# Latent attention with the rope query's high and low parts stacked in one operand and half of its heads' rope made in the loop; forgetting attention with padded keys and the decay added by VectorE

## The chip, the cores and the metric

The kernel runs on one core of one Trainium2 chip. The metric is the device time of one execution in microseconds; lower is better. The engines have queues of their own: PE (TensorE, matrix products, with its weight loads listed as PEld), DVE (VectorE), ACT (ScalarE), POOL (GpSimd) and SP (SyncE, which only issues DMAs here). An engine runs its queue in order, and an instruction waits at the head of its queue until what it reads is there.

## The reference, cut to what matters

The program is a decoder trunk of two layers on 256 tokens of width 1024, all in float32. A layer is: half a SwiGLU feed-forward (2816 wide), an attention mixer, another half feed-forward, and a gated per-layer embedding, each followed by a layer norm. Layer 0's mixer is forgetting attention (FoX, 16 heads of 64), layer 1's is latent attention (MLA, 16 heads, 128 numbers without position and 64 rotated by rope, with one rotated key for all heads).

```python
def fox_mixer(x, w_in, b_f, w_o):
    h = x @ w_in                                  # q, k, v and one gate logit a head
    cum = jnp.cumsum(jax.nn.log_sigmoid(f_logit), axis=1).transpose(0, 2, 1)
    ...
        s = jnp.einsum('bqhd,bkhd->bhqk', qb, k).astype(jnp.float32) * scale
        return s + cb[:, :, :, None] - cum[:, :, None, :]

def mla_mixer(x, w_dq, q_norm, w_uq, w_o, k_nope, k_rope, v, cos, sin):
    c_q = rms_norm(x @ w_dq, q_norm)
    q = jnp.einsum('bsc,chd->bshd', c_q, w_uq)
    q_nope = q[..., :QK_NOPE_DIM]
    q_rope = rope(q[..., QK_NOPE_DIM:], cos[:, None, :], sin[:, None, :])
    ...
        s = jnp.einsum('bqhd,bkhd->bhqk', qn, k_nope) + jnp.einsum('bqhr,bkr->bhqk', qr, k_rope)
```

Softmax over the keys up to the query's own place follows, then the product with v and with w_o.

## The kernel before, in words

**Precision by parts.** PE works on float32r operands. Every operand is held as a high part (an ACT copy to float32r) and a low part (a DVE subtraction of the high part from the source); `parts` makes such a pair, and `mm3` forms a product as three matmuls into one PSUM bank: high by high, high by low, low by high.

**Weights.** `Stream` loads weights of HBM by DMA from the SP queue into three raw buffers, up to three groups ahead, and splits each piece into its parts in one of about ten buffers (`hl`, and `ota`, `otb`, `qk`, `fs` when they are lent). A split of 1024 columns is one ACT and one DVE instruction (lines 164 and 165). The order of everything is the order in which the Python code emits it; the only planner is `pump`, which after each product emits the next split if its own clock says that ACT and DVE are free. `S.hold` turns it off.

**FoX.** Heads go in pairs, j = 0 to 7. `gen_k(j)` and `gen_q(j)` make the pair's keys and queries (24 matmuls each), head 0 in partitions 0 to 63 and head 1 in 64 to 127. `QK(j)` has a bank for each head: first a product with `sel` and `negc` that adds minus 8 times the decay of the keys, and then six matmuls a head with 64 partitions each. `softmax(j)` adds the causal mask and takes the row's maximum on DVE (line 954), corrects it by the query's decay `cq` (two small DVE instructions a head), takes the exponentials on ACT and divides on POOL. `T(j)` transposes the weights on PE, `AV(j)` multiplies with v. The decays come from `gates()`: a product and then a chain of ACT, POOL and DVE steps, emitted one by one (`bg`) whenever a weight is used. The iteration j is: gen_k(j+1), T(j-1), QK(j), softmax(j), gen_q(j+1), AV(j-1).

**MLA.** Ahead of the loop over heads stand `dq(t)` (the query latent of token block t, then its norm), `V(g, t)` (values of four heads), `cq_transpose(t)`, `q_rope(t)` (the 16 heads' rope queries of block t: two banks, 18 matmuls, then three DVE instructions and an addition on POOL or DVE a bank), `transposed` (eight PE transposes of them and their parts into `xT`), and `gen(0)`, `gen(1)` (`gen` makes a head's key and query without position). The loop over heads h is: gen(h+1), T(h-1), QK(h), softmax(h), O(h-2), at some heads V, AV(h-1). `QK(h)` is an `mm3` on `qk` and an `mm3` on the rope parts `xT` and `kr`, for queries 0 to 127 (128 keys) and 128 to 255 (256 keys). The rope operands hold two heads in their 128 partitions; `kr[s]` is zero in the other head's half. `softmax(h)` takes the maximum (line 1263) and the exponentials (line 1267), and emits the division (POOL, line 1274) at once; `O` is the output product. PSUM has rings of banks: `y` (4), `h` (2), `tr` (2); QK and T share `tr`, gen, AV and V share `h`.

Of the kernel before, what the change touches and what calls it, by code (L numbers as in the profile page):

```python
# [52 lines left out]
VT = {0: (2, (0,)), 5: (2, (1,)), 8: (3, (0,)), 10: (3, (1,))}  # L53
# [201 lines left out]
WIDTH = {"kd": 1280, "dq": 1536, "kq": 1280, "kvv": 1024, "ff": 1024}  # L255


def group_of(key):
    k = key[0]
    if k in ("win", "fv", "kd", "dq"):  # L260
        return key[:-1] + (key[-1] // 2,)
    if k in ("wout", "fk", "fq", "fo", "pg", "pp", "mo", "qr"):
        return key[:-1] + (key[-1] // 2,)
    if k in ("kvk", "qn"):
        return ("kq", key[-1])
    return key


def unit_of(key, raw):
# [4 lines left out]
    if k in ("wout", "fo", "pg", "pp", "mo", "qr"):  # L274
        return raw[:, 1024 * u : 1024 * u + 1024], 128, 1024
# [17 lines left out]
def make_loads(a):  # L293
# [3 lines left out]
    def loads(q, g, raw, fine, between):  # L297
# [41 lines left out]
        elif k == "qr":  # L339
            w = a["mla_w_uq"][0]  # L340
            for s in range(2):
                kk = 2 * i + s
                if kk < 3:
                    q.dma_start(
                        raw[:, 1024 * s : 1024 * s + 1024].rearrange("p (h d) -> p h d", d=64),
                        w[128 * kk : 128 * kk + 128, :, 128:192],
                    )
# [31 lines left out]
class Trunk:  # L379
    def __init__(self, nc, pools, a, S, rec):  # L380
        self.nc, self.a, self.S = nc, a, S
        self.sb, self.ps = pools
        self.rec = rec
        self.bg = deque()
        self.setup()
# [418 lines left out]
    def fox(self, li):  # L804
# [26 lines left out]
        bf = self.tl([128, 1], F32, "bf", 1)  # L831
        sel = self.tl([128, 16], F32R, "sel", 1)
        negc = self.tl([128, 384], F32R, "negc", 1)
        cq = self.tl([128, 16, 2], F32, "cq", 1)
        fr = slice(96, 128)
        nc.gpsimd.memset(bf, 0.0)
        if not self.rec:
            self.dma(bf[112:128, :], a["fox_b_f"][0].rearrange("(p o) -> p o", o=1))
        nc.gpsimd.memset(fs, 0.0)
        nc.gpsimd.memset(negc.bitcast(F32), 0.0)  # L840
        sf = fs[:, 1792:1808]
        nc.gpsimd.tensor_tensor(sf, self.ident[:, 16:32], self.ident[:, 48:64], op=ALU.add)
        nc.gpsimd.tensor_tensor(sf, sf, self.ident[:, 80:96], op=ALU.add)
        nc.gpsimd.tensor_tensor(sel, sf, self.ident[:, 112:128], op=ALU.add)
# [3 lines left out]
        m8 = fs[fr, 1536:1792]  # L848

        def gates():  # L850
# [3 lines left out]
            def s1():  # L854
                nc.scalar.activation(f, ps[fr, 0:256], AF.Identity, bias=bf[fr, :])
                nc.scalar.activation(ab, f, AF.Abs)
# [6 lines left out]
            def s2():  # L863
# [3 lines left out]
                nc.gpsimd.tensor_tensor(u, e, ab, op=ALU.subtract)  # L867
# [3 lines left out]
            def s3():  # L871
                nc.vector.scalar_tensor_tensor(f, f, 0.0, u, op0=ALU.min, op1=ALU.add)
                nc.vector.tensor_tensor_scan(sc[fr, :], f, r, 0.0, op0=ALU.add, op1=ALU.add)
                nc.gpsimd.tensor_scalar(m8, sc[fr, :], -8.0, 1.0, op0=ALU.mult, op1=ALU.mult)
                self.S.busy(dve=600)

            def s4():
                nc.scalar.activation(negc[fr, 0:128], m8[:, 0:128], AF.Copy)
                nc.scalar.activation(negc[fr, 128:384], m8, AF.Copy)

            def s5():
                nc.vector.tensor_tensor(
                    negc[64:96, 128:384], m8, negc[fr, 128:384].bitcast(F32), op=ALU.subtract
                )
                nc.vector.tensor_copy(negc[64:96, 0:128], negc[64:96, 128:256].bitcast(F32))
                self.S.busy(dve=400)

            def s6():
                nc.vector.tensor_copy(negc[0:64, :], negc[64:128, :].bitcast(F32))

            rest = lambda: None
            self.bg.extend((s1, rest, rest, s2, rest, rest, s3, rest, s4, s5, s6))

        def gates_transpose():
            tr = self.bank("tr")
            for t in range(2):
                self.transpose(tr[:, 128 * t : 128 * t + 128], sc[:, 128 * t : 128 * t + 128])
            nc.vector.tensor_copy(
                cq.rearrange("p h t -> p t h"),
                tr[:, 0:256].rearrange("p (t c) -> p t c", c=128)[:, :, 112:128],  # L900
            )
# [8 lines left out]
        qk = self.own([128, 2, 2, 512], F32R, "qk")  # L910
        OT = [self.own([128, 4, 2, 256], F32R, tag) for tag in ("ota", "otb")]

        def gen(j, key, c0, at={}, hold=False):
            ps = self.bank("h")
            ws((key, j), ps[:, 0:256], at, hold)
            o = qk[:, j % 2]
            self.parts(o[:, 0, c0 : c0 + 256], o[:, 1, c0 : c0 + 256], ps[:, 0:256])

        def gen_k(j):
            gen(j, "fk", 256, {0: S.split_now} if j >= 2 else {}, j >= 2)  # L920

        def gen_q(j):
            gen(j, "fq", 0, {}, j >= 2)

        def QK(j, ring):
            sb = [self.bank(ring) for _ in range(2)]
            half = [slice(0, 64), slice(64, 128)]
            o = qk[:, j % 2]
            for s in range(2):
                h = 2 * j + s  # L930
                self.mm(
                    sb[s][:, 0:384], sel[half[s], h : h + 1].to_broadcast([64, 128]), negc[half[s], :],
                    True, False,
                )
            for n, (i, jj) in enumerate(((0, 0), (0, 1), (1, 0))):
                for q0, c0, c1 in ((0, 0, 128), (128, 128, 384)):
                    for s in range(2):
                        self.mm(
                            sb[s][:, c0:c1], o[half[s], i, q0 : q0 + 128],
# [509 lines left out]
```

## Time and profile before

| | |
|---|---|
| median of 3 runs | 1095.18 us (1095.08 to 1095.76) |
| the profiled execution | 1095.58 us, its span from the first to the last instruction 1093.6 us, the other 2.0 us lie around it |
| granted TensorE clock | 0.997 of full speed |
| PE busy | 98% of the span |
| FoX, about | 198 to 312 us of the span |
| MLA, about | 717 to 872 us of the span |

A row of the timeline gives the start, the time that the row covers, engine, line, operation, out<-in, shapes and how many instructions it merges; behind it in brackets stands how long its engine had been idle and what ended that. Matmuls are pipelined: the end of one overlaps the start of the next, so what a matmul costs is read from start to start.

### The profile page before, as it was taken

The page shows a single profiled execution, that of the slowest core. Times are in us where ns is not written, and L with a number is a line of the kernel's source. Part 1 is how long each engine was busy: PE and PEld are TensorE (multiplying, and loading weights), DVE is VectorE, ACT ScalarE, POOL GpSimd, SP SyncE. Part 2 cuts the span into 40 slices and gives each one's busy share as a digit, 9 for nine tenths or more (in the row PEclk, how much of TensorE's full clock was granted, in tenths as well). Part 3 has the DMA queues.
Part 4 walks back from the last instruction along what each step waited for, and adds up shares of the span by engine and source line. Part 5 has one row for each costly group of instructions (what it writes and reads, how often), then busy time and mean ns, then how long its engine had stood idle before and what let it go on. Part 6 is the DMA issues. An engine that isn't in the chain of part 4 may idle for free. (4 is left out here: it accounts for less than half of the span.)

```text
span 1093.6 us, 17616 instructions
## 1 busy us (share of the span) xinstructions
PE 1072.9 (98%) x7148; PEld 970.6 (89%) x7148; DVE 712.1 (65%) x1010; ACT 539.3 (49%) x787; POOL 81.3 (7%) x129
## 2 busy tenths in 40 slices
PE   9999999999999999999999999998999999999996
PEld 6989999899889999988899899987899789898985
DVE  5765545788797545449976454487766886454567
ACT  5564433666645444443664353345655474344431
POOL 0000000322200000001420000011111000000000
PEclk9999999999999999999999999999999999999998
DMA  8896652444358866545577664353533678555502
GB/s 276 279 297 225 205 186 92 155 154 156 119 173 286 269 210 198 187 140 164 171 257 266 193 193 148 103 145 113 155 116 116 202 257 294 165 192 192 192 1 77
DMA packets 150960, 200.04 MB, mean 183 GB/s; under 512 B 11872, under 2 KB 128608, under 8 KB 150880
## 3 DMA queue, kind: packets, MB, share of 16 engines
q1 hardware_dynamic: 150880, 198.92, 56.1%
q8 instruction: 56, 0.92, 0.3%
q14 instruction: 24, 0.20, 0.1%
HBM read 197.85 MB, written 1.05 MB: 182 GB/s over the span
## 5 line engine op out<-in xcount | busy, mean ns | idle before, releaser
L165 DVE TENSOR_TENSOR hl<-raw,hl 128x1024 fp32r<-128x1024 f32 (+3 forms) x285 | 331.6, 1182 | 172.9 <-ACT hl L164 172.0
L164 ACT ACTIVATE hl<-raw 128x1024 fp32r<-128x1024 f32 (+3 forms) x285 | 284.4, 1019 | 197.5 <-PE y L464 83.3
L464 PE MATMUL h<-xT,hl 128*128 128x256 f32 x2064 | 243.7, 278 | 1.0 <-DVE qk L474 0.6
L464 PEld LDWEIGHTS h<-xT,hl 128*128 128x128 f32 x2064 | 238.3, 188 | 2.4 <-DVE qk L474 0.8
L464 PE MATMUL y<-hl,g 128*128 128x512 f32 x804 | 186.6, 390 | 0.0
L464 PEld LDWEIGHTS y<-hl,g 128*128 128x128 f32 x804 | 150.1, 188 | 30.7
L464 PE MATMUL tr<-xT,hl 128*128 128x256 f32 x840 | 98.9, 277 | 0.0
L464 PEld LDWEIGHTS tr<-xT,hl 128*128 128x128 f32 x840 | 96.9, 188 | 0.1
L464 PE MATMUL h<-hl,xT 128*128 128x512 f32 (+1 forms) x396 | 95.1, 389 | 1.1 <-DVE hl L165 0.9
L464 PEld LDWEIGHTS h<-hl,xT 128*128 128x128 f32 x396 | 71.9, 188 | 17.9 <-DVE hl L165 3.4
L536 POOL TENSOR_TENSOR rs<-ve,mhalf 128x1 f32<-128x1 f32 x16 | 14.8, 923 | 822.7 <-DVE ve L535 809.1
L464 PE MATMUL y<-hl,xT 128*128 128x512 f32 (+2 forms) x276 | 57.8, 363 | 0.0
L464 PEld LDWEIGHTS y<-hl,xT 128*128 128x128 f32 x276 | 47.5, 188 | 7.4
L474 DVE TENSOR_TENSOR g<-P,g 128x512 fp32r<-128x512 f32 x36 | 24.9, 693 | 34.4 <-ACT g L473 34.4
L473 ACT ACTIVATE g<-P 128x512 fp32r<-128x512 f32 x36 | 22.7, 632 | 39.9 <-DVE P L643 29.0
L473 ACT ACTIVATE xT<-tr 128x512 fp32r<-128x512 f32 x36 | 20.0, 596 | 37.3 <-PE tr L468 37.1
L464 PE MATMUL y<-hl,ota 128*128 128x512 f32 x144 | 36.1, 394 | 0.0
L165 DVE TENSOR_TENSOR otb<-raw,otb 128x1024 fp32r<-128x1024 f32 (+1 forms) x20 | 24.1, 1203 | 18.2 <-ACT otb L164 18.2
L165 DVE TENSOR_TENSOR qk<-raw,qk 128x1024 fp32r<-128x1024 f32 x21 | 25.7, 1224 | 15.4 <-ACT qk L164 15.4
L164 ACT ACTIVATE qk<-raw 128x1024 fp32r<-128x1024 f32 x21 | 22.2, 1058 | 19.3 <-PE tr L464 6.6
L464 PE MATMUL tr<-xT,otb 128*128 128x256 f32 x264 | 31.7, 276 | 0.0
L464 PEld LDWEIGHTS tr<-xT,otb 128*128 128x128 f32 x264 | 30.7, 188 | 0.0
(230 smaller groups left out, 1374.7 us busy)
## 6 DMA issues: line engine op xcount, KB each, us to landing
raw<-in_ffn_w_in_dram SPq DMA_DIRECT2D x172, 512.0 KB, 4.9
raw<-in_ffn_w_out_dram SPq DMA_DIRECT2D x44, 1024.0 KB, 5.2
raw<-in_fox_w_in_dram SPq DMA_DIRECT2D x12, 1024.0 KB, 5.2
raw<-in_ple_w_gate_dram SPq DMA_DIRECT2D x8, 1024.0 KB, 5.1
raw<-in_mla_w_o_dram SPq DMA_DIRECT2D x8, 1024.0 KB, 5.1
gb<-in_ln_g_dram SPq DMA_DIRECT2D x8, 512.0 KB, 7.3
gb<-in_ln_b_dram SPq DMA_DIRECT2D x8, 512.0 KB, 8.1
raw<-in_fox_w_o_dram SPq DMA_DIRECT2D x4, 1024.0 KB, 5.0
```

Of the source, the lines that this page charges most:

```text
L164: nc.scalar.activation(hi[:, c], src[:, c], AF.Copy)
L165: nc.vector.tensor_tensor(lo[:, c], src[:, c], hi[:, c].bitcast(F32), op=ALU.subtract)
L464: self.nc.tensor.matmul(out, lhsT, rhs, start=start, stop=stop)
L473: self.nc.scalar.activation(hi, src, AF.Copy)
L474: self.nc.vector.tensor_tensor(lo, src, hi.bitcast(F32), op=ALU.subtract)
L536: nc.gpsimd.tensor_tensor(rs, ve, self.mhalf, op=ALU.pow)
```

## The change

**MLA.** The rope query's operand now holds, for one head, its high part in one half of the partitions and its low part in the other; the key's high part stands in both halves (`kr[0]`), its low part in one (`kr[1]`, `kr[2]`), so that the rope product takes two matmuls instead of three. `q_rope` works by token block and half of the heads (n): heads 0 to 7 ahead of the loop, heads 8 to 15 inside it (products at h = 0 and 1, `rotate` behind them, transposes `rope_T` at h = 3 and 5). The weights for it are loaded in other groups. In the loop, gen(h+1) and T(h-1) now stand behind QK(h) and its maxima; the exponentials, the low part of T's copy and the division follow separately, and `S.hold` keeps weight splits out until gen(h+1) is emitted. V(1,0) uses the `y` ring, V(2) is made ahead of the loop, V(3) at h = 7 and 9, and the layer norm's gain is loaded at h = 9. The latent query (`cqt`) lies in `fall`'s buffer.

**FoX.** The key operand `kz` has a zero half for each head, so that a query of both heads (`qq`, 128 partitions) gives one head's scores: QK is six matmuls with 128 partitions into two banks. The decay no longer goes through PE: `gates()` ends by storing 8 times the cumulated decay in DRAM (`decay`), from which four broadcast DMAs fill `fall` (four heads each); `mask_fall` applies the causal mask on POOL, and the DVE instruction of the maximum adds `fall` or `tri` instead of the mask. `sel`, `negc`, `cq` and their instructions go, and the two reciprocals of a pair become one.

```diff
-            self.bg.extend((s1, rest, rest, s2, rest, rest, s3, rest, s4, s5, s6))
...
+                self.dma(decay, sc[112:128, :])
+                load_fall(0)
+                load_fall(1)
+                mask_fall(0)
+            self.bg.extend((s1, rest, s2, rest, rest, s3))
+        def load_fall(g):
+            if not self.rec:
+                d = decay[4 * g : 4 * g + 4, :]
+                self.dma(
+                    fall[:, g % 2].rearrange("p h c -> p (h c)"),
+                    bass.AP(tensor=d.tensor, offset=d.offset, ap=[[0, 128], [1, 1024]]),
+                )
+        def mask_fall(j):
+            h = slice(2 * (j % 2), 2 * (j % 2) + 2)
+            a, b = fall[:, j // 2 % 2, h], tri[:, j // 2 % 2, h]
+            for out, src in ((b, a[:, :, 0:128]), (a[:, :, 128:256], a[:, :, 128:256])):
+                nc.gpsimd.affine_select(
...
         def QK(j, ring):
             sb = [self.bank(ring) for _ in range(2)]
-            for s in range(2):
-                h = 2 * j + s
+            q, k = qq[:, j % 2], kz[:, j % 2]
+            pairs = lambda ap: ap.rearrange("p (s c) -> p s c", s=2)
+            for n, (i, jj) in enumerate(((0, 0), (0, 1), (1, 0))):
                 self.mm(
-                    sb[s][:, 0:384], sel[half[s], h : h + 1].to_broadcast([64, 128]), negc[half[s], :],
-                    True, False,
+                    pairs(sb[0][:, 0:256]), q[:, i, 0:128], pairs(k[:, jj])[:, :, 0:128], n == 0, n == 2
                 )
             for n, (i, jj) in enumerate(((0, 0), (0, 1), (1, 0))):
-                for q0, c0, c1 in ((0, 0, 128), (128, 128, 384)):
-                    for s in range(2):
-                        self.mm(
-                            sb[s][:, c0:c1], o[half[s], i, q0 : q0 + 128],
-                            o[half[s], jj, 256 : 256 + c1 - c0], False, n == 2 and q0 > 0,
-                        )
+                self.mm(sb[1], q[:, i, 128:256], k[:, jj], n == 0, n == 2)
...
+        def rope_T(t, n, ring="tr"):
+            tr = self.bank(ring)
+            for i in range(4):
+                self.transpose(tr[:, 128 * i : 128 * i + 128], z[n][t][:, 128 * i : 128 * i + 128])
+            src = tr.rearrange("p (k c) -> p k c", c=128)
+            half = [slice(64 * s, 64 * s + 64) for s in range(2)]
+            o = [self.xT[:, t, s, 4 * n : 4 * n + 4, :] for s in range(2)]
+            for s in range(2):
+                nc.scalar.activation(o[s][half[s]], src[half[s]], AF.Copy)
+            for s in range(2):
+                nc.vector.tensor_tensor(
+                    o[s][half[1 - s]], src[half[s]], o[s][half[s]].bitcast(F32), op=ALU.subtract
+                )
...
-                self.mm3(
-                    b[:, c0:c1], lambda i: self.xT[:, q0 // 128, i, pair, :],
-                    lambda i: kr[:, i, 0:w], False, True,
-                )
+                r = self.xT[:, q0 // 128, h % 2, h // 2, :]
+                self.mm(b[:, c0:c1], r, self.kr[0][:, 0:w], False, False)
+                self.mm(b[:, c0:c1], r, self.kr[1 + h % 2][:, 0:w], False, True)
...
         for h in range(16):
-            if 1 <= h < 15:
+            S.hold = True
+            QK(h)
+            softmax(h)
+            if h >= 1:
+                T(h - 1)
+            exps(h)
+            if h >= 1:
+                T_low(h - 1)
+            divide(h)
+            if h == 0:
+                gen_q(1)
+            elif h < 15:
                 gen(h + 1)
+            S.hold = False
+            if h == 0:
+                q_rope(0, 1)
+            if h == 1:
+                rotate(0, 1)
+                q_rope(1, 1)
...
+            if h in (3, 5):
+                rope_T(h // 2 - 1, 1, "h")
+            if h in VT:
+                V(*VT[h])
+            if h == 9:
+                self.load_gb(li, 1)
             if h == 15:
                 S.lend("qk")
                 O(LATE, (1,))
-            if h >= 1:
-                T(h - 1)
-            QK(h)
-            softmax(h)
             if h >= 2:
                 O(h - 2, (0, 1) if h - 2 < LATE else (0,))
...
             if h >= 1:
                 AV(h - 1)
+            if h == 1:
+                rotate(1, 1)
```

The next rows are instruction queues in the order in which the program holds them (line, operation, out<-in, shape of the output, how many in a row); the number behind a name counts buffers. First PE in MLA, ahead of the loop, before: `gb` is the latent query's buffer, `ota` the rotated rope queries, `tr<-qk` and `tr<-fs,xT` are QK(0), whose rope keys lie in `fs`.

```order
L464 MATMUL y<-hl_7096,gb 128x512 x6
L468 MATMUL tr<-ident,ota 128x128 x8
L464 MATMUL h<-fs,hl_7111 128x256 x6
L464 MATMUL h<-gb,hl_7125 128x256 x9
L464 MATMUL h<-hl_6949,fs 128x512 x6
L468 MATMUL tr<-ident,ota 128x128 x8
L464 MATMUL h<-fs,hl_7111 128x256 x6
L464 MATMUL h<-gb,hl_7125 128x256 x9
L464 MATMUL tr<-qk 128x128 x3
L464 MATMUL tr<-fs,xT 128x128 x3
L464 MATMUL tr<-qk 128x256 x3
L464 MATMUL tr<-fs,xT 128x256 x3
```

The same stretch of PE in the changed program, where `fall` is the latent query's buffer:

```order
L467 MATMUL h<-fs,hl_7036 128x256 x12
L467 MATMUL y<-hl_6928,fall 128x512 x6
L467 MATMUL y<-hl_7005,fall 128x512 x3
L467 MATMUL h<-fall,hl_7050 128x256 x9
L471 MATMUL tr<-ident,ota 128x128 x4
L467 MATMUL y<-hl_7064,fs 128x512 x6
L471 MATMUL tr<-ident,ota 128x128 x4
L467 MATMUL y<-hl_7064,fs 128x512 x6
L467 MATMUL tr<-qk 128x128 x3
L467 MATMUL tr<-fs,xT 128x128 x2
L467 MATMUL tr<-qk 128x256 x3
L467 MATMUL tr<-fs,xT 128x256 x2
```

The transposes of the rope queries (`tr<-ident,ota`) are 8 instead of 16 and have a product of V behind each four, the gen of head 0 stands ahead of them, gen(1)'s query has moved behind QK(0), and QK(0)'s rope rows are 2 and 2 instead of 3 and 3.

Now DVE in the loop, around head 2, before: the first four rows are softmax(2)'s maxima, `su` the division's reciprocal, `hl` are weight splits, `ota` is AV(1)'s low part, `qk` the low part of gen(4), `PT` that of T(2).

```order
L1263 ISA tr,nm<-tr,mask 128x128
L1263 ISA nm 128x1
L1263 ISA tr,nm<-tr,mask 128x256
L1263 ISA nm 128x1
L1272 RECIPROCAL su<-su 128x2
L165 TENSOR_TENSOR hl_7469<-raw,hl_7469 128x1024
L165 TENSOR_TENSOR hl_7484<-raw,hl_7484 128x512
L474 TENSOR_TENSOR ota<-h,ota 128x256
L165 TENSOR_TENSOR hl_7497<-raw,hl_7497 128x768
L165 TENSOR_TENSOR hl_7508<-raw,hl_7508 128x1024
L474 TENSOR_TENSOR qk<-h,qk 128x512
L474 TENSOR_TENSOR PT<-tr,PT 128x384
```

The same engine in the changed program around head 2:

```order
L1288 ISA tr,nm<-tr,mask 128x128
L1288 ISA nm 128x1
L1288 ISA tr,nm<-tr,mask 128x256
L1288 ISA nm 128x1
L1322 TENSOR_TENSOR PT<-tr,PT 128x384
L1305 RECIPROCAL su<-su 128x2
L477 TENSOR_TENSOR qk<-h,qk 128x512
L165 TENSOR_TENSOR hl_7403<-raw,hl_7403 128x512
L165 TENSOR_TENSOR hl_7409<-raw,hl_7409 128x768
L165 TENSOR_TENSOR hl_7420<-raw,hl_7420 128x1024
L477 TENSOR_TENSOR ota<-h,ota 128x256
```

`PT` (T(1)'s low part) now stands between the maxima and the reciprocal, the low part of `qk` is that of the next head, gen(3), behind this head's reciprocal instead of a head ahead, and the splits come behind it.

Last PE in FoX, around QK of a pair in the loop, before: `tr<-ident,P` is T of the pair before, `y<-negc,sel` and `y<-qk` are QK, `h<-xT` is a gen.

```order
L991 MATMUL tr<-ident,P 128x128 x4
L468 MATMUL tr<-ident,P 128x128 x2
L464 MATMUL y<-negc,sel 128x384 x2
L464 MATMUL y<-qk 128x128 x2
L464 MATMUL y<-qk 128x256 x2
L464 MATMUL y<-qk 128x128 x2
L464 MATMUL y<-qk 128x256 x2
L464 MATMUL y<-qk 128x128 x2
L464 MATMUL y<-qk 128x256 x2
L464 MATMUL h<-xT,hl_2051 128x256 x24
```

And the same PE rows in the changed program, where `qk` holds the padded keys and `qq` the queries:

```order
L986 MATMUL tr<-ident,P 128x128 x4
L471 MATMUL tr<-ident,P 128x128 x2
L467 MATMUL y<-qk,qq 128x256 x3
L467 MATMUL y<-qk,qq 128x512 x3
L467 MATMUL h<-xT,hl_2059 128x256 x24
```

The two products with `negc` and the twelve of 64 partitions have become three of 256 columns and three of 512.

More of the change, by code (lines that the diff above doesn't have):

```diff
@@ L909, in fox, with gen_k @@
         st, PT = {}, {}
-        qk = self.own([128, 2, 2, 512], F32R, "qk")
         OT = [self.own([128, 4, 2, 256], F32R, tag) for tag in ("ota", "otb")]
-        def gen(j, key, c0, at={}, hold=False):
+        def gen_k(j):
             ps = self.bank("h")
[L915 to L920, printed above, removed]
+            ws(("fk", j), ps[:, 0:256], {0: S.split_now} if j >= 2 else {}, j >= 2)
+            o = kz[:, j % 2]
+            part = [(slice(64 * s, 64 * s + 64), slice(256 * s, 256 * s + 256)) for s in range(2)]
+            for r, c in part:
+                nc.scalar.activation(o[r, 0, c], ps[r, 0:256], AF.Copy)
+            for r, c in part:
+                nc.vector.tensor_tensor(o[r, 1, c], ps[r, 0:256], o[r, 0, c].bitcast(F32), op=ALU.subtract)
+            self.S.busy(act=600, dve=600)
```

260 lines of the change are left out of this document (138 added, 122 removed).

## The prediction

> **What bounds the kernel now.** I read the page's engine sums first, then busy time by stretch, then PE's waits, and last the timeline at each wait.
>
> ```profile
> span 1093.6 us, 17616 instructions
> PE 1072.9 (98%) x7148; PEld 970.6 (89%) x7148; DVE 712.1 (65%) x1010; ACT 539.3 (49%) x787; POOL 81.3 (7%) x129
> ```
>
> PE is busy for 98% of the span, so only two things shorten the kernel: fewer or shorter matmuls, and the removal of the few waits of PE. DVE, at 65%, is next. The two stretches of latent attention are where PE is not full (stretch, its length, then us busy and instructions of PE, its weight loads, DVE, ACT and POOL, the granted clock, the DMA engines' busy share, GB/s):
>
> ```profile
> 716.70:748.00 31.30, 28.85 (x155) 24.25 (x155) 28.66 (x47) 14.59 (x26) 6.02 (x7) 1.00 0.57 165
> 748.00:859.00 111.00, 106.44 (x730) 96.57 (x730) 74.56 (x165) 66.71 (x148) 13.63 (x32) 1.00 0.40 123
> ```
>
> The first is MLA ahead of its loop, the second the loop: 2.5 and 4.6 us without PE work. In the first DVE is busy for 28.7 of 31.3 us, so there DVE sets the pace with PE; in the loop it has a third of its time left. What PE waits for in MLA (total, times, longest):
>
> ```profile
> PE tr L468 <- POOL P L1274: 1.7, 3, 0.8
> PE tr L464 <- DVE g L474: 1.2, 1, 1.2
> PE tr L468 <- DVE xT L474: 1.2, 1, 1.2
> PE h L464 <- DVE PT L474: 1.1, 1, 1.1
> PE tr L468 <- DVE PT L1166: 0.8, 1, 0.8
> PE h L464 <- DVE g L474: 0.4, 1, 0.4
> ```
>
> A wait costs more than the idle time listed, since the pipeline runs empty:
>
> ```profile
> 743.98 1.55 PE L464 MATMUL h<-hl,fs 128*128 128x512 f32 x6
> 746.71 1.16 PE L468 MATMUL tr<-ident,ota 128*128 128x128 f32 x8 [1.18 <-DVE xT L474]
> ```
>
> Six matmuls of 512 columns take 6 x 0.233 us from start to start (next fence), so the transposes could have begun at 745.38 and began at 746.71: 1.33 lost for 1.18 idle. I add 0.15 us to each wait.
>
> **MLA, rope product: -3.7 us.** The price of a matmul is read from start to start in QK(0):
>
> ```profile
> 749.69 0.45 PE L464 MATMUL tr<-qk 128*128 128x128 f32 x3
> 749.98 0.50 PE L464 MATMUL tr<-fs,xT 128*128 128x128 f32 x3
> 750.32 0.57 PE L464 MATMUL tr<-qk 128*128 128x256 f32 x3
> 750.72 0.51 PE L464 MATMUL tr<-fs,xT 128*128 128x256 f32 x3
> 751.07 1.56 PE L464 MATMUL tr<-hl,fs 128*128 128x512 f32 x6
> 752.47 0.87 PE L464 MATMUL h<-fs,hl 128*128 128x256 f32 x6
> ```
>
> Three of 128 columns on the rope operands take 0.34 us, three of 256 take 0.35, six of 512 take 1.40: 0.113, 0.117 and 0.233 each. A head loses one of the first and one of the second: 0.23 us, times 16 heads 3.7 us, all on the full engine.
>
> **FoX, QK: -1.6 us.** A pair of heads in the loop before:
>
> ```profile
> 243.47 0.38 PE L468 MATMUL tr<-ident,P 128*128 128x128 f32 x2
> 243.78 0.44 PE L464 MATMUL y<-negc,sel 64*128 64x384 f32 x2
> 244.06 0.85 PE L464 MATMUL y<-qk 64*128 64x128 f32 x12
> 244.84 0.39 PE L464 MATMUL h<-xT,hl 128*128 128x256 f32 x1
> ```
>
> QK takes 244.84 - 243.78 = 1.06 us, and the two transposes ahead of it 0.31, where two at 0.113 would take 0.23: about 0.1 us is lost when PE goes from 128 to 64 partitions, and perhaps as much on the way back, which no row shows by itself. After: three of 256 and three of 512, 3 x 0.117 + 3 x 0.233 = 1.05 us, and no switch. The gain a pair lies between 0.1 (one switch) and 0.2 (both); I take 0.2, since the trace has both switches, so 8 x 0.2 = 1.6 us. The Trainium skill, "TensorEngine Tiling (Array Packing)", Theoretical Speedup, says that a contraction of 64 or less may run up to two times faster as row tiles. By that rule the 3072 columns (2 x 384 and 12 of 128 or 256) should take half of 3072 x 0.455 ns, 0.70 us, the padded form would cost 0.35 us more a pair, and the sum below would end 4.4 us higher. The trace disagrees in size: 1.06 us. The same page says that a change of tiling mode drains the engine (Key Properties); the 0.1 us agree.
>
> The two transposes of `gates_transpose` go as well: -0.3 us by the 0.31 above.
>
> **FoX, the start: about zero.** PE waits there once for the low part of gen(0), queued on DVE:
>
> ```profile
> 224.71 0.50 PE L464 MATMUL h<-xT,hl 128*128 128x256 f32 x2 [0.60 <-DVE qk L474]
> 219.22 0.69 DVE L873 TENSOR_TENSOR_SCAN fs<-fs 32x256 f32<-32x256 f32 x1
> 229.02 0.30 DVE L954 CUSTOM_DVE_ANT_0 y<-y,mask 128x128 f32<-128x128 f32 x1 [0.34 <-PE y L464]
> 232.96 1.63 POOL L976 TENSOR_SCALAR P<-P,su 128x128 f32<-128x128 f32 x4 [11.52 <-DVE su L973]
> 234.49 0.60 PE L991 MATMUL tr<-ident,P 128*128 128x128 f32 x4
> ```
>
> The three DVE steps that build `negc` go, so the 0.6 + 0.15 goes: -0.8. In its place stands a new wait. The maxima of pair 0 (229.02) now need `fall`: the scan's end, the store of `decay`, a broadcast load and two masks on POOL. The nearest DMAs and the nearest mask:
>
> ```profile
> bf<-in_fox_b_f_dram SPq DMA_DIRECT2D x1, 0.1 KB, 1.5
> DMA to landing us min/median/max: 4.0/7.7/9.7
> L437 POOL TENSOR_SCALAR_AFFINE_SELECT mask<-mask x2: 292/293/294, 4.2 to 4.4; 128x128 f32<-128x128 f32 x2
> ```
>
> The second row is that of the sixteen `gb` loads, which also broadcast 512 KB. The scan ends at 219.9 now; the steps between are emitted one weight use earlier, so 1.4 us earlier at best. 218.5 to 219.9, plus 1.5 to 2, plus 4.0 to 9.7, plus 2 x 0.6 (twice the mask's columns): 225.2 to 232.8. PE will end QK(0) near 228 (its wait and two transposes are gone). So the delay is 0 to 4.8 us; the middle, a load of 6 to 7 us, gives about 1, which I take. It reaches PE at once: T(0) begins at 234.49 while POOL ends its divisions at 234.59. The other three loads have a whole pair (8.5 us) or more. On SP the store and the loads stand between weight loads, which then wait for the scan; FoX needs 1 MB in some 8 us, and three buffers cover that. The masks take POOL 1.2 us a pair beside 1.6 of division: hidden. gen_k's parts become two ACT and two DVE instructions, the correction by `cq` (four) goes: even, and hidden under PE. Sum of the start: -0.8 + 1.0.
>
> **MLA, ahead of the loop: -2.5 us.** V(1,0) in the `y` ring no longer waits for a bank: -0.4 - 0.15. cq_transpose(1) has 15 matmuls of 512 (3.4 us) behind dq(1) instead of 12 (2.7), and the wait was 0.8 + 0.15: about -0.9. The rope transposes wait 1.33 for the bank that DVE empties late; now a V product (1.4 us) stands behind each four, and half of the DVE work of rope is left to the loop: -1.3. Fewer waits mean that PE comes sooner to what DVE makes, and DVE is nearly full here; q_rope(1,0) will meet the low part of the second `cqt` late. I give back 0.3 (bounds 0 and 1.5, about what DVE works ahead today): -0.6 - 0.9 - 1.3 + 0.3. The rope weights come in six DMAs instead of three, with the same bytes, on queues that are busy for 0.57 of the stretch.
>
> **MLA, the loop: -3.2 us.** T(1) before:
>
> ```profile
> 760.90 0.82 POOL L1274 TENSOR_SCALAR P<-P,su 128x128 f32<-128x128 f32 x2 [6.38 <-DVE su L1272]
> 761.32 0.89 PE L468 MATMUL tr<-ident,P 128*128 128x128 f32 x3 [0.78 <-POOL P L1274]
> 768.68 0.49 PE L468 MATMUL tr<-ident,P 128*128 128x128 f32 x3
> 756.25 0.55 PE L464 MATMUL tr<-qk 128*128 128x128 f32 x3 [1.24 <-DVE g L474]
> 858.27 0.79 PE L464 MATMUL h<-PT,g 128*128 128x256 f32 x5 [1.06 <-DVE PT L474]
> ```
>
> T that waits for the division also crawls (0.89 for 0.49). With QK(h) ahead of it T has 1.2 us more: the three waits go, 1.7 + 3 x 0.15 + 3 x 0.4 = -3.3. The wait of QK(1) for V's bank (756.25) goes: -1.4. AV(15)'s (858.27) is DVE's backlog of splits behind O and stays in part: -0.7. What is late next is QK(h+1), since its query and key are now made after the exponentials of h on ACT and its reciprocal on DVE:
>
> ```profile
> 758.65 0.29 DVE L1263 CUSTOM_DVE_ANT_0 tr<-tr,mask 128x128 f32<-128x128 f32 x1
> 761.72 0.60 ACT L473 ACTIVATE qk<-h 128x512 fp32r<-128x512 f32 x1
> 763.00 0.68 DVE L474 TENSOR_TENSOR qk<-h,qk 128x512 fp32r<-128x512 f32 x1
> 754.37 1.23 DVE L165 TENSOR_TENSOR hl<-raw,hl 128x1024 fp32r<-128x1024 f32 x1 [0.78 <-ACT hl L164]
> 739.50 0.68 DVE L1214 TENSOR_TENSOR ota<-y,rope 128x512 f32<-128x512 f32 x1
> ```
>
> From the first maximum to the division are 760.90 - 758.65 = 2.25 us, then ACT's 0.6 and DVE's 0.7: 3.5 us. PE has T, gen, O and AV between two QK: 0.35 + 15 x 0.117 + 12 x 0.233 + 0.7 = 5.6 us. So a head's maxima may begin 2 us late on DVE before PE waits. In a plain head DVE has some 2 us of splits there and is in time. In h = 0 to 5 it also gets rope: six instructions (1.5 us a bank) and four of 0.7. At h = 0 there is no O and no AV, so QK(1) waits about 1.0, and I allow 1.2 for h = 2 to 5. Loop: -3.3 - 1.4 - 0.7 + 1.0 + 1.2 = -3.2, with bounds of 0 (every wait comes back) and -6.4 (none of the new ones, AV(15)'s gone). V(3) at h = 7 and 9 adds what V at 5, 8 and 10 no longer does; the gain's load at h = 9 is two DMAs that nobody waits for on PE.
>
> **Sum.** -3.7 - 1.6 - 0.3 + 0.2 - 2.5 - 3.2 = -11.1. The profiled execution took 1095.58 us, 0.4 above the median; 1095.58 - 11.1 = 1084.5, and 1084.1 against the median. I give 1084.
>
> **Rivals.** *The waits move on.* DVE is nearly full ahead of the loop and gets rope's rest in the first heads; if all of MLA's waits come back as waits for `qk` and `cqt`, only the matmuls stay: -3.7 - 1.6 - 0.3, and FoX's start between -0.8 and +2: 1089 to 1092. For it speaks the new chain through ACT and DVE, against it the 2 us of slack in a plain head. The tiling rule of the skill would put the result here too, with the gains ahead of the loop halved.
>
> *Slower.* QK(h+1) waits in every head. It decides at one point: how late a head's maxima begin on DVE. Up to 2.0 us cost nothing; at 3.2 us (three splits, 1.23 each, ahead of them, less the 0.5 in which PE waits for AV) each of 15 heads loses 1.2 us, 18 in all, against 11 gained: 1102. Against it: the splits of two heads are four (3 to 4 us), not six, so such a head is followed by a lighter one.
>
> *`fall` comes late.* A load of 9.7 us makes T(0) wait 4.8 instead of 1: 1088. For it: two loads issued together.
>
> *The rope's rest in the loop is free*: without the 2.2 us of new waits there and with AV(15)'s wait gone, 1081.
>
> **How the numbers follow.** About 0.2%, 2.2 us, can be told from no change. Forecast (1079.5 to 1088, with `fall` late or rope free at its ends): 0.68. Waits move on (1088 to 1093): 0.18. Within 0.2%: 0.05. Slower: 0.04. More gain than that of 1079.5: 0.05. The range of 8 in 10 goes from 1079.5 to 1090. Faster by over 0.2%: 0.91.
>
> **What would show it.** In the changed trace: QK of FoX 1.05 us from start to start, no `negc`; the rope rows of a head two and two, 0.23 us each; no wait of T for POOL; a wait of `tr<-qk` for `qk` in the first heads of at most 1 us each; T(0) of FoX waiting for POOL by about 1 us. I am wrong if PE waits for `qk` in most of the sixteen heads, or if weight splits held back by `S.hold` make gen wait for `hl`.

## The result and the profile after

The changed kernel takes 1081.55 us in the median (1080.49 to 1082.38, 4 runs) against 1095.13 us beside it (1094.57 to 1095.76): a ratio of 0.9878, 95% interval 0.9866 to 0.9891. The prediction was 1084.0 us, range 1079.5 to 1090. The gain is 13.6 us where 11.1 were forecast. Head of the page of the changed kernel:

```profile
span 1078.7 us, 17453 instructions
PE 1064.0 (99%) x7050; PEld 966.6 (90%) x7050; DVE 711.2 (66%) x979; ACT 541.8 (50%) x797; POOL 86.9 (8%) x143
```

PE's busy time fell by 8.9 us of the 14.9 by which the span of the profiled execution shrank; the other 6.0 were idle time, and PE is now at 99%. The two stretches of latent attention, ahead of its loop and in it, with the columns of the first table of the prediction:

```profile
714.00:741.00 27.00, 27.00 (x150) 23.72 (x149) 25.18 (x41) 14.27 (x26) 3.44 (x5) 1.00 0.60 163
741.00:846.00 105.00, 104.04 (x713) 95.62 (x712) 82.34 (x177) 70.34 (x156) 16.70 (x34) 1.00 0.49 155
```

PE had 2.5 us idle in the first of them before, and has none; 4.6 in the second, and has 1.0. DVE went the other way in the loop, from 74.6 of 111 us to 82.3 of 105: rope's second half is there now. PE's waits in attention (total, times, longest):

```profile
PE tr L986 <- POOL P L973: 1.1, 1, 1.1
PE tr L467 <- ACT qk L476: 0.6, 1, 0.6
PE tr L467 <- DVE qk L477: 0.4, 1, 0.4
```

The first is T(0) of forgetting attention; the other two lie in one and the same product, QK(1) of latent attention. All six waits that the prediction listed for latent attention are gone. QK(0), by starts, and the wait of QK(1):

```profile
741.38 0.39 PE L467 MATMUL tr<-fs,xT 128*128 128x128 f32 x2
741.61 0.56 PE L467 MATMUL tr<-qk 128*128 128x256 f32 x3
742.01 0.40 PE L467 MATMUL tr<-fs,xT 128*128 128x256 f32 x2
742.25 1.23 PE L467 MATMUL h<-fall,hl 128*128 128x256 f32 x9
743.32 2.27 PE L467 MATMUL y<-hl,fall 128*128 128x512 f32 x9
746.15 0.33 PE L467 MATMUL tr<-qk 128*128 128x128 f32 x1 [0.56 <-ACT qk L476]
746.88 0.33 PE L467 MATMUL tr<-qk 128*128 128x128 f32 x1 [0.40 <-DVE qk L477]
748.02 0.49 PE L471 MATMUL tr<-ident,P 128*128 128x128 f32 x3
```

Two rope matmuls of 128 columns take 0.23 us (741.38 to 741.61), two of 256 take 0.24. T(0), the last row, runs at full speed.

Where the 14.9 us between the two profiled spans (1093.6 and 1078.7) lie, counted between the transposes of the layer's input (`tr<-ident,x`, XT(0) and XT(1) for its two token blocks): 1.1 ahead of forgetting attention, where nothing was changed; 0.9 from XT(1) to XT(0) in forgetting attention (107.86 to 106.93 us); 12.3 from the XT(0) ahead of latent attention to the one at its end (154.01 to 141.70 us); 0.6 behind it, again unchanged code.

### The profile page after: what moved, and what is told of

It reads as the page before. It is cut to its first block, busy times and chain, and to the rows that moved or that the text cites. A ratio compares the mean times of both kernels' runs of the same rounds, so it can differ in the third digit from the quotient of the medians.

```text
span 1078.7 us, 17453 instructions
## 1 busy us (share of the span) xinstructions
PE 1064.0 (99%) x7050; PEld 966.6 (90%) x7050; DVE 711.2 (66%) x979; ACT 541.8 (50%) x797; POOL 86.9 (8%) x143
## 3 DMA queue, kind: packets, MB, share of 16 engines
HBM read 199.95 MB, written 1.06 MB: 186 GB/s over the span
## 5 line engine op out<-in xcount | busy, mean ns | idle before, releaser
L476 ACT ACTIVATE xT<-tr 128x512 fp32r<-128x512 f32 x32 | 17.8, 595 | 31.7 <-PE tr L471 31.4
L164 ACT ACTIVATE otb<-raw 128x1024 fp32r<-128x1024 f32 (+1 forms) x20 | 20.8, 1040 | 21.0 <-PE tr L467 10.6
```

The source lines that it names most:

```text
L164: nc.scalar.activation(hi[:, c], src[:, c], AF.Copy)
L476: self.nc.scalar.activation(hi, src, AF.Copy)
```

## The experiments

The changes of time are against the kernel before (ratio with its 95% interval) and, where it matters, against the changed kernel's 1081.55. Profiles are compared by the same stretches: FoX for XT(1) to XT(0) in forgetting attention, MLA for XT(0) to XT(0) around latent attention.

### The two parts alone

The function `fox` of one kernel put into the other, with what it needs of pools.

> The changed latent attention with forgetting attention as before. If the two parts add up as the stretches of the two traces say (154.01 to 141.70 us in latent attention, 0.6 behind it), this is 12.3 to 12.9 us faster than before, about 1082.5 us. If my prediction's sizes were right and the rest of the 13.6 us came from elsewhere, it is 9.4 us faster, about 1085.7.

> The changed forgetting attention with latent attention as before. By the trace's stretch from 201 to 309 us it is 0.9 us faster, about 1094.2 us: 8 pairs by 0.21 us won and about 1 us given back at the first pair's maxima. By my prediction's sum 1.7 us faster, 1093.4. If two row tiles ran at twice the speed before, it would be about 2.7 us slower by the sum, 1097.8.

Latent attention alone: 1081.57 us, 0.9878 (0.9865 to 0.9892), MLA 141.61 us. Forgetting attention alone: 1093.90 us, 0.9994 (0.9985 to 1.0003), FoX 106.88 us. So latent attention makes the gain; forgetting attention's 0.9 us stand in the trace only, below what a timing of it resolves. Had the products of 64 partitions run at twice the speed before, it would be 1097.8 us; that is excluded.

### A third rope matmul

```diff
-                self.mm(b[:, c0:c1], r, self.kr[1 + h % 2][:, 0:w], False, True)
+                self.mm(b[:, c0:c1], r, self.kr[1 + h % 2][:, 0:w], False, False)
+                self.mm(b[:, c0:c1], r, self.kr[2 - h % 2][:, 0:w], False, True)
```

> The changed kernel with a third rope matmul in each product of latent attention (the low half of the queries times the low half of the keys, a term that both kernels leave out). If a matmul is paid in full, 0.113 + 0.117 us in each of 16 heads, 3.7 us slower than the changed kernel, about 1085.2 us. If the rope matmuls lie in the shade of a wait in some heads (the wait of QK(1) alone does not hide them, since they come behind it), less: nothing would mean that DVE sets the loop's pace, 1081.5.

1084.65 us, 0.9909 (0.9895 to 0.9922): 3.1 us more, and 3.1 in MLA. A late head of this kernel:

```profile
821.33 0.50 PE L467 MATMUL tr<-fs,xT 128*128 128x128 f32 x3
821.66 0.57 PE L467 MATMUL tr<-qk 128*128 128x256 f32 x3
822.07 0.52 PE L467 MATMUL tr<-fs,xT 128*128 128x256 f32 x3
822.43 0.49 PE L471 MATMUL tr<-ident,P 128*128 128x128 f32 x3
```

Three and three where the changed kernel has two and two, 0.33 and 0.36 us by starts; from QK to QK a late head takes 5.56 us instead of 5.34. The 0.22 are paid in full, 3.5 in 16 heads; the wait of QK(1) took in part of the rest (QK to QK of head 0 is 5.05 us with and 5.04 without).

### T ahead of QK again, in the changed kernel

```diff
-            QK(h); softmax(h)
             if h >= 1:
-                T(h - 1)
-            exps(h)
-            if h >= 1:
-                T_low(h - 1)
-            divide(h)
+                T(h - 1); T_low(h - 1)
+            QK(h); softmax(h); exps(h); divide(h)
```

> The changed kernel with T(h-1) put back ahead of QK(h), as before, everything else as changed. If the place of T is what removed its waits, T waits for POOL again in the heads where DVE is late, in three heads 3.3 us as before: 1083.5 to 1085. If the rest of the change (fewer matmuls, rope's rest elsewhere) removed them, or QK(h+1) now waits less because the maxima come no later, it stays at 1081.5, and the trace shows no wait of T.

1086.23 us, 0.9923 (0.9911 to 0.9936): 4.7 us more, MLA 146.65. PE's own list has 1.3 us of waits of T, that of its weight loads (PEld) 4.4; the third row is T of head 4:

```profile
PE tr L471 <- POOL P L1307: 1.3, 2, 0.8
PEld tr L471 <- POOL P L1307: 4.4, 10, 1.3
775.20 0.89 PE L471 MATMUL tr<-ident,P 128*128 128x128 f32 x3
```

In seven heads T's three transposes take nearly 0.4 us more, as this row against the 0.49 above: the weight load of the second, which reads what POOL divides, waits 0.32 us for POOL's second division, and three of the seven had waited for the first division too. By the starts, about 4.5 us are lost at T, as the list of the weight loads says, and QK(1) no longer loses its own 1.35; the rest of the 4.95 us of MLA, about 1.8, is lost in O, V, AV and the rope transposes. Both theories set it too low; that the place of T removes its waits in the changed kernel is shown.

### QK ahead of T alone, in the kernel before

The opposite edit: in the kernel before, QK(h) and its maxima ahead of T(h-1), exponentials between T's high and low part, nothing else. The changed kernel also puts gen(h+1) behind QK(h) and T(h-1); here it stays ahead of them.

> The kernel before with nothing changed but the order in latent attention's loop: QK(h) and its maxima ahead of T(h-1), the exponentials between T's high and low part. If the place of T alone removed its waits, the 3.8 us that T loses in the trace before go: 1091.1 us, with no new wait, since query and key are still made a head ahead. If T's waits only move to QK, whose bank of scores is now asked for earlier, 1094 to 1095.

1094.50 us, 1.0001 (0.9992 to 1.001), MLA 153.88: no gain. T's waits for POOL are gone from its trace, and in their place stand:

```profile
PE h L464 <- DVE PT L1297: 2.5, 2, 1.7
PE h L464 <- ACT PT L1292: 0.6, 1, 0.6
758.13 0.78 PE L464 MATMUL h<-PT,g 128*128 128x256 f32 x5 [1.70 <-DVE PT L1297]
760.00:762.00 2.00, 2.00 (x12) 2.00 (x11) 1.23 (x1) 0.38 (x2) 0.00 (x0) 0.50 0.70 281
```

The listed waits of PE in latent attention sum to 5.8 us where they were 6.4, and the stretch is 0.1 us shorter. Not QK waits, as the rival had it, though its time is right, but AV: with no O in head 1 yet, AV(0) follows T(0) at once and waits for T's parts. Behind that wait PE also runs at half its rate for some microseconds (granted clock, the third column from the end, 0.50 in the last row): by the starts gen and QK(2) lose 1.4 us to it, so that part of "no gain" is the clock. In the changed kernel gen(2), 15 matmuls (748.26 to 750.13), and q_rope(1,1), nine (750.13 to 752.22), stand between T(0) and AV(0).

So the place of QK and T alone is not enough: with rope in the loop but T first, T waits (4.7 us); with only QK ahead of T, AV waits. Whether gen behind T would cover AV's wait without rope's half in the loop is not shown: no run has the one without the other.

### All of rope ahead of the loop again

```diff
         gen_q(0)
+        q_rope(0, 1); rotate(0, 1)
         rope_T(0, 0)
...
+        q_rope(1, 1); rotate(1, 1); rope_T(0, 1)
         V(2, 1, "y", "qq")
+        rope_T(1, 1)
```

> The changed kernel with the second half of the rope queries made ahead of the loop again. The PE work is the same. If DVE set the pace ahead of the loop before, its 6.9 us of rope work come back there and PE waits for DVE at the rope transposes and at QK(0), 1.5 to 3 us slower, 1083 to 1084.5. If the half in the loop only moved the same waits, it stays at 1081.5; the wait of QK(1), 1.35 us, may also shrink.

1097.34 us (1094.26 to 1099.22), 1.0016 (1.0007 to 1.0026): 15.8 us more, far above what I expected. PE by the timeline, and two windows (granted clock in the third column from the end):

```profile
748.93 0.93 PE L471 MATMUL tr<-ident,gb 128*128 128x128 f32 x4 [2.10 <-POOL gb L1219]
749.51 0.88 PE L467 MATMUL tr<-qk 128*128 128x128 f32 x3
750.20 0.63 PE L467 MATMUL tr<-fs,xT 128*128 128x128 f32 x2
754.92 0.33 PE L467 MATMUL tr<-qk 128*128 128x128 f32 x1 [1.54 <-ACT qk L476]
771.73 0.50 PE L467 MATMUL y<-hl,ota 128*128 128x512 f32 x1 [1.63 <-ACT hl L164]
745.00:757.00 12.00, 7.96 (x41) 7.00 (x40) 7.68 (x16) 5.65 (x11) 2.10 (x3) 0.82 0.00 1
757.00:770.00 13.00, 11.16 (x55) 10.36 (x54) 5.42 (x15) 4.30 (x13) 1.65 (x4) 0.64 0.24 81
```

Three costs are mixed. The rope transposes and QK(1) wait, as expected. Then gen and O wait for weights (`hl`): my kernel held their splits back for the longer stretch, and the loads behind them stopped (DMA share 0.00). And behind a wait of 2.1 us PE runs slower: three matmuls of 128 columns take 0.69 us by starts (749.51 to 750.20) instead of 0.34, at a granted clock of 0.82 and 0.64 in these windows. To take the second cost out:

```diff
+        S.hold = False
         q_rope(0, 1); rotate(0, 1)
```

> As the kernel with all of rope ahead of the loop, but weights are split there from the second half of rope on, as they are in the changed loop. If the held-back splits made most of the 15.8 us (gen and O waited for weights), 1083 to 1086 us: the waits at the rope transposes and at QK(1), 4.6 us in that trace, partly stay. If DVE is simply too full ahead of the loop for rope and splits, the waits grow there instead and it stays above 1090.

1090.21 us, 0.9950 (0.9938 to 0.9963): 8.7 us more than the changed kernel, MLA 150.73. The waits for weights are gone, 7.1 us of the 15.8 (some of it clock); these are left, the two longest waits of PE in latent attention, and then the window ahead of the loop:

```profile
PE tr L467 <- ACT qk L476: 2.8, 1, 2.8
PE tr L471 <- POOL gb L1219: 2.6, 1, 2.6
714.00:750.50 36.50, 33.53 (x184) 28.65 (x183) 34.34 (x56) 19.37 (x33) 6.51 (x7) 1.00 0.55 153
```

The first theory's range, 1083 to 1086, is missed too; the second, DVE too full and the waits longer, holds. DVE is busy for 34.3 of 36.5 us ahead of the loop, so what is late there is late at QK(0), and with the new order QK(1) waits behind it. By the starts the last rope transposes lose 2.8 us, QK(1) 2.3 more than in the changed kernel, QK(2) 0.6, and 3.0 go to matmuls at half rate behind the wait of QK(1) (granted clock 0.50 from 756 to 760 us): 8.7 of the 9.0 us in MLA. So the half in the loop is worth more than the 1.3 us that the prediction gave the rope transposes, even without the clock.

### How late may the maxima come

```diff
+            for _ in range({10: 2, 12: 4, 14: 6}.get(h, 0)):
+                nc.vector.tensor_tensor(Pt[:, 384:768], self.mask, self.mask, op=ALU.add)
```

> The changed kernel with extra DVE work (additions of 384 columns into an unused part of P, about 0.5 us each) ahead of the maxima of heads 10, 12 and 14: two, four and six of them, about 1.0, 2.0 and 3.1 us. By my prediction maxima may come 2.0 us late before QK of the next head waits: 0, 0 and 1.1 us lost. By the changed kernel's trace the late heads, where O covers one half only, have about 0.7 us (low parts of head h+1 end 0.5 us ahead of QK(h+1), exponentials 0.2 us ahead of the high parts): 0.3, 1.3 and 2.4 us lost.

One run, so its trace decides and not its time: 1087.48 us. MLA is 145.49, 3.8 us over the changed kernel's: the second theory's sum (4.0), not the prediction's (1.1). Of the rest of the time 1.8 us lie in forgetting attention, which this edit does not touch. QK(15), behind the additions of head 14:

```profile
840.13 0.33 PE L467 MATMUL tr<-qk 128*128 128x128 f32 x1 [0.29 <-ACT qk L476]
```

Counted from the head's QK, the maxima came 1.0, 1.8 and 2.9 us later than in the changed kernel, and each time the next QK waited: by the starts QK(11) loses 0.4 us, QK(13) 1.0, QK(15) with the AV ahead of it 1.5. QK(14), behind a head without additions, loses another 0.6, and those 0.6 are also in the 2.9. Why so little is free, a late head of the changed kernel tells, with its high part, low part and QK:

```profile
821.70 0.60 ACT L476 ACTIVATE qk<-h 128x512 fp32r<-128x512 f32 x1 [0.22 <-PE h L467]
822.33 0.69 DVE L477 TENSOR_TENSOR qk<-h,qk 128x512 fp32r<-128x512 f32 x1 [0.59 <-ACT qk L476]
823.52 0.50 PE L467 MATMUL tr<-qk 128*128 128x128 f32 x3
```

ACT is 0.22 us idle before the high part and the low part ends 0.50 before QK: 0.7 us in all. From head 8 on O covers one half of the tokens, so PE needs 5.34 us a head and not 6.7; the 2.0 us of the prediction hold for the earlier heads only, where maxima come up to 1.9 us late and cost nothing.

### The held-back split in forgetting attention

```diff
-            S.later()
             nc.vector.reciprocal(su, su)
...
+            S.later()
```

> The changed kernel with the held-back low part of a weight split put behind the divisions of forgetting attention, as it was before. If the last division of the first pair took 1.44 us instead of 0.48 because the split's DVE instruction ran beside it, POOL's four divisions take 1.63 us again and T(0) ends 1.0 us earlier: 1080.5 us. If the slow division has another cause, nothing changes, 1081.5.

1082.70 us (1081.86 to 1083.64), 0.9890 (0.9877 to 0.9904): not faster, FoX 107.83 instead of 106.93. T(0) waits as long as before, since the split runs beside POOL's last division either way; and now a division is slowed in pairs 1 to 6 too, where in the changed kernel it was not. Pair 3, POOL's four divisions, the split's low part on DVE, T on PE, first here and then in the changed kernel (POOL, PE):

```profile
257.87 2.50 POOL L972 TENSOR_SCALAR P<-P,su 128x128 f32<-128x128 f32 x4 [4.35 <-DVE su L968]
257.68 1.20 DVE L176 TENSOR_TENSOR hl<-raw,hl 128x1024 fp32r<-128x1024 f32 x1
259.91 0.84 PE L986 MATMUL tr<-ident,P 128*128 128x128 f32 x4
```

```profile
256.97 1.62 POOL L973 TENSOR_SCALAR P<-P,su 128x128 f32<-128x128 f32 x4 [4.90 <-DVE su L969]
259.35 0.60 PE L986 MATMUL tr<-ident,P 128*128 128x128 f32 x4
```

The direction was wrong and the cause right: a division beside the split waits for the split's end, 0.9 us. So POOL's four divisions end at 260.4, and T, which reaches PE at 259.9, pays 0.25 to 0.35 us in each of four pairs. The Trainium skill, "SBUF — State Buffer", section "SBUF: two separate sides", says that DVE with two SBUF inputs and a GpSimd instruction that reads SBUF lock each other out for a whole instruction. The traces agree: the split (both inputs in SBUF) blocks; the query's low part (one input in PSUM), at 231.98 in the fence of the next section, ran beside a division that took its usual 0.37 us.

### ACT's table and QK(1): two small edits on the changed kernel

The start of forgetting attention in the changed kernel, on POOL, ACT and DVE:

```profile
226.92 0.41 POOL L898 TENSOR_SCALAR_AFFINE_SELECT tri<-fall 128x256 f32<-128x256 f32 x1 [9.16 <-DMA fall<-decay]
226.63 0.86 DVE L920 TENSOR_TENSOR qk<-h,qk 64x256 fp32r<-64x256 f32 x2 [0.95 <-ACT qk L918]
228.66 1.28 ACT L962 ACT_TABLE_LOAD   x1 [2.06 <-DVE nm L952]
231.99 2.59 POOL L973 TENSOR_SCALAR P<-P,su 128x128 f32<-128x128 f32 x4 [4.29 <-DVE su L969]
231.98 0.42 DVE L477 TENSOR_TENSOR qq<-h,qq 128x256 fp32r<-128x256 f32 x1
232.92 1.31 DVE L176 TENSOR_TENSOR hl<-raw,hl 128x1024 fp32r<-128x1024 f32 x1 [0.52 <-ACT hl L172]
234.63 0.33 PE L986 MATMUL tr<-ident,P 128*128 128x128 f32 x1 [1.08 <-POOL P L973]
```

Behind the scan (`s3`), one exponential of one column, so that the table is loaded there:

```diff
+                warm = self.tl([128, 1], F32, "ss", 2)
+                nc.scalar.activation(warm, self.mhalf, AF.Exp)
```

> The changed kernel with one small exponential on ACT right behind the scan of forgetting attention, so that ACT's table for exponentials is loaded there and not behind the first maxima (1.28 us, from 228.66 to 229.94 in the changed trace). If that load is on the path to T(0), which lost 2.2 us, all but some 0.3 us of the loss go: 1079.6 us. If POOL's last division, slowed by DVE's split, still ends last at the old time, about 0.5 us or less: 1081.

1079.67 us, 0.9858 (0.9843 to 0.9873), FoX 105.76, 1.2 below the changed kernel's. The exponentials come 1.3 us earlier (counted from XT(1)) and T(0) still waits 0.8 us for POOL, whose divisions again take 2.60: in the trace it lies between the two expectations; the time is 1.9 us below the changed kernel's, more than this stretch explains. "ScalarE: Activation LUTs" of the Trainium skill, section "What ACT_TABLE_LOAD costs", gives 1283 ns for the load and about 1380 for a drain. The trace shows the first (1.28) and not the second: the exponential starts at 229.95, 0.01 us behind the load.

The second edit makes the parts of V(2,0) and V(2,1) behind the maxima of head 0, the first behind softmax(0), the second behind gen_q(1), and had the same early exponential in latent attention, behind gen_q(0):

```diff
-        split_v = V(2, 0, "y", later=True)
+        split_0 = V(2, 0, "y", later=True)
...
-        V(2, 1, "y", "qq")
+        split_1 = V(2, 1, "y", "qq", later=True)
...
+            if h == 0: split_0()
...
+                split_1()
```

> The changed kernel with the low parts of V(2,0) and V(2,1) put behind the maxima of head 0 and ACT's table for exponentials loaded earlier. If the wait of QK(1), 1.35 us, comes from DVE's queue ahead of the maxima and from that load, it goes: 1080.2 us. If the chain from QK(0) through exponentials to the query's low part is too long by itself with only gen_q(1) and q_rope(0,1) on PE, at least half of the wait stays: 1081.

1081.74 us, 0.9878 (0.9865 to 0.9892): nothing. QK(1) no longer waits, QK(0) does:

```profile
738.66 1.28 ACT L1378 ACT_TABLE_LOAD   x1
742.82 0.52 PE L467 MATMUL tr<-qk 128*128 128x128 f32 x3 [1.18 <-DVE xT L1232]
```

The load now stands on ACT ahead of the rope queries, which QK(0) needs. Without the extra exponential, and with the one in forgetting attention:

> The early table load in forgetting attention, and the low parts of V(2,0) and V(2,1) behind the maxima of head 0 without an extra exponential in latent attention. If the late QK(0) of the kernel with the low parts moved came from that extra table load on ACT ahead of the rope queries, QK(0) is on time here, QK(1) waits 0 to 0.3 us instead of 1.35, and the time is 1.1 to 1.3 us below the kernel with the early table load: 1078.4 to 1078.6 us. If the wait of QK(1) moves again, to QK(0) or to QK(2), 1079.5.

1079.28 us (1078.99 to 1079.57), 0.9854 (0.9838 to 0.9871). QK(0) is on time and QK(1) has no wait:

```profile
744.66 0.69 PE L467 MATMUL tr<-qk 128*128 128x128 f32 x3
```

MLA is 140.95 us, 0.75 below the changed kernel's: part of the 1.35 is given back in the heads with rope, 0.2 to 0.3 us from QK to QK in two of them. This version's four runs lie below all four of the changed kernel, by 2.3 us in the median, though the two were not timed side by side; the traces account for 1.9 (FoX 1.16, MLA 0.75). By its interval it is not told from the version with the table load alone.

## Why the prediction was right, and where it was off

The time was in the range, and the mechanism was that of the forecast; four terms had a wrong size. That the sum came out within 2.5 us of the measured 13.6 owes something to luck: the start of forgetting attention came out about 1 us worse than forecast, latent attention 2 to 3 us better.

- **Rope product, -3.7.** Right: 0.23 us a head by the starts, 0.22 a head in the late heads with the third matmul.
- **QK of forgetting attention, -1.6.** Right in sum: from QK to QK of a pair 8.54 us became 8.33, 1.7 in eight. By the starts it is made up otherwise. The pair at which the prediction read 243.47 to 244.84, in the changed kernel:

```profile
243.14 0.38 PE L471 MATMUL tr<-ident,P 128*128 128x128 f32 x2
243.27 1.29 PE L467 MATMUL y<-qk,qq 128*128 128x256 f32 x6
244.40 2.89 PE L467 MATMUL h<-xT,hl 128*128 128x256 f32 x24
```

  QK itself went from 1.06 to about 1.13 us, and the two transposes ahead of it from 0.31 to 0.13 (all six from 0.75 to 0.57). The loss on entering the 64-partition form was thus nearer 0.2 than the 0.1 that I read, since I took 0.113 for a transpose. The other 0.1 of a pair lies in one of its two gens (2.72 us instead of 2.84), unchanged code; why is open. Twice the speed is excluded, but the form did gain: at the prediction's prices on the full array the 14 matmuls of the old QK would take about 1.7 us (an estimate), and they took 1.06.
- **The start of forgetting attention, +0.2.** With the -0.3 of `gates_transpose`, which lies in the same stretch, the forecast is -0.1. The trace has +0.8 (+1.0 without the 0.2 of QK's own term): QK(0) comes 1.2 us earlier (0.8 and 0.3 expected), but from QK(0) to QK(1) 7.38 us became 9.32. I blamed `fall` and priced its load at 6 to 7 us; the page has

```profile
fall<-decay SPq DMA_DIRECT2D x4, 512.0 KB, 4.2
decay<-fs SPq DMA_DIRECT2D x1, 16.0 KB, 3.7
```

  The load is 2 us shorter than taken and the store 2 us longer. The first maximum came 1.9 us behind QK(0)'s start where it was 1.2: +0.7, near my 1, but by luck. `fall` was not what it waited for: its mask had ended at 227.33, while DVE worked on gen_k(1)'s low parts until 227.49 (the row `qk<-h,qk` above) and began the maximum at 227.52. I had called those parts "even, and hidden under PE". What I left out besides is POOL's division. One reciprocal for both heads lets it begin only behind the last exponential (exponentials' end to division's end: 1.3 us before, 3.0 after), and the lock with DVE is 1.0 of these 3.0. The step that failed is the price of this start: it takes the 1.6 us of division as given ("the masks take POOL 1.2 us a pair beside 1.6 of division: hidden"), with no word on the order of reciprocal and split.
- **Ahead of the loop, -2.5.** -3.1 by the starts (losses of more than 0.12 us: 3.4 before, 0.3 after). The 0.3 that I gave back did not come: q_rope(1,0) does not wait for the second `cqt`; twelve other matmuls (`h<-fs,hl`) stand ahead of it, which may be why.
- **The loop, -3.2.** -4.9 by the same count. T gave 3.8 (3.3 taken; in the trace before, the weight loads of T list 4.4 us of waits for POOL where PE lists 1.7), the bank of V 1.4, AV(15) 1.1 (0.7 taken: its loss is 0.17). QK(1) cost 1.35 (1.0 taken). QK(2) to QK(5) cost nothing where I took 1.2, the largest error: maxima come up to 1.8 us late there and the 2.0 us that I had worked out myself cover it. That part of the rival "the rope's rest in the loop is free", 1081, is what happened.
- **The rival "slower".** It was nearer than I said. I gave every head 2.0 us; the late ones have 0.7. What kept it away, by these figures, is that rope's work is in the early heads; no run puts it into the late ones.
- **"The waits move on."** It did not happen to this change; it did to QK ahead of T alone and to the first form of the QK(1) edit.

Open: the 1.1 us ahead of forgetting attention and the 0.6 behind latent attention, in unchanged code; kernels here differ there by as much between profiled executions, and no run was made for it. In the first kernel with rope ahead of the loop the slower clock is not taken apart from the waits. Why the clock falls behind one wait and not behind another is open too.

## What to carry to other kernels

A wait that is removed by order alone can go to the next consumer unless other PE work stands where it would appear; look for that work first. Read slack in the trace from the producer's end to the consumer's start, head by head, and not from one average head. PE's list of idle times shows only part of a wait in the middle of short matmuls (1.3 us of about 4.5 here); the list of its weight loads, PEld, shows it (4.4).

## What the runs showed of the hardware

- Behind a wait of 2.1 us PE ran at half its rate for some microseconds (matmuls of 128 columns at 0.21 us instead of 0.11), but not behind one of 2.6 us in the next kernel, where the four rope matmuls of QK(0) ran at full rate; there it came behind the wait of 2.8. In the kernel with QK ahead of T alone it came behind waits of 0.6 and 1.7 us with one matmul between them. "TensorE: Matmul & The Clock Gate" of the Trainium skill, Part 1, has PE fall to half its clock after at least one idle window of about 3.4 us, which is free-running. That it is half the clock agrees (granted 0.50); the length does not, since it fell here behind shorter waits. No wait of the changed kernel is over 1.2 us, and its two stretches in the first section show a clock of 1.00.
- POOL's divisions and DVE's weight splits exclude each other: 0.48 us became 1.44 for a division of 256 columns beside a split of 1.31.
- A store of 16 KB to DRAM took 3.7 us from issue to landing, nearly as long as a broadcast load of 512 KB (4.2).
